# Dividing attention outputs instead of attention weights in a hybrid RWKV-7 / MLA trunk

## The chip, the cores and the metric

The kernel runs on one core of one Trainium2 chip. The core has five engines that run side by side and wait for one another through semaphores: PE (TensorE, matrix products and transposes through the array, results in PSUM), DVE (VectorE), ACT (ScalarE), POOL (GpSimd) and SP (SyncE, which here issues the DMA transfers). In the profile PEld is the loading of weights into the array, which overlaps PE's products. The metric is device time in microseconds; the time before is the median of three runs.

## The reference, cut to what matters

Two layers of a decoder trunk over 512 tokens, width 1024. Each layer projects the normed input, runs an RWKV-7 time mix and an MLA attention beside each other, gates and sums both, and adds a gated ConvFFN. The change lies in the attention of MLA, 8 heads with values of width 64:

```
def attend(args):                      # one block of 128 queries
    qn, qr, q0 = args
    s = (jnp.einsum('bqhd,bkhd->bhqk', qn, k_nope)
         + jnp.einsum('bqhr,bkr->bhqk', qr, k_pe)).astype(jnp.float32) * scale
    q_pos = q0 + jnp.arange(Q_BLOCK, dtype=jnp.int32)
    s = jnp.where(key_pos[None, :] <= q_pos[:, None], s, NEG_INF)
    p = jax.nn.softmax(s, axis=-1).astype(v.dtype)
    return jnp.einsum('bhqk,bkhd->bqhd', p, v)
...
y_b = MLA(p_B) @ w_out_mla
merged = sigmoid(gate_a) * y_a + sigmoid(gate_b) * y_b
```

## The kernel before

All activations are kept transposed: 128 features on the partitions, 512 tokens along a row. Weights stream from HBM in units of eight 128x128 tiles (raw); ACT rounds each to a high part (whi, L201) and DVE takes the rest (wlo, L202), and every large product is three matmuls of 512 columns, high by high, high by low and low by high (mm3, L246 to L248, into an accumulator acc). split (L276 to L284) makes the same two parts, hi on ACT (L279) and lo on DVE (L280), of an activation that such a product is to read.

The mixer of a layer has three stages. The first projects the input. The second is the RWKV scan over eight chunks (L777 to L815), whose matmuls on PE stand in an order written out by hand. The third, in pool tb (from L817), has six parts, listed at L952: outputs makes the four output blocks of the scan (chunk_out, L825, copied out of the PSUM tile xy on ACT, L844); norms does a group norm on each (L848 to L863: sums, subtraction and squares on DVE and ACT, the power on POOL at L858, the scaling on POOL at L863); heads(0) and heads(1) do the attention of two pairs of heads; transposed turns the normed blocks into operands of the next product (yop, L867, PE transposes at L869, then a split); heads(2) and heads(3) do the other two pairs. Behind them come eight products with the operands yops (wtile, L957, 12 matmuls each, read by DVE at L960), and after the mixer eight products with the attention operands oops (L978, read at L981).

Outside of the blocks marked manual_schedule a planner sets the order of the instructions on each engine, from the dependencies, the order of the program, its own estimate of how long each one takes, and the buffers that are free. So the engines do not run these parts one after the other: in the trace heads(0) begins among the last chunks of the scan, heads(1) runs among the group norms, and the products with yops fill gaps of heads(2) and heads(3). An engine then takes its instructions strictly in the order that the planner gave it.

heads(p) (L907 to L950) works like this. K of the pair is projected (L909) and copied for each of its two heads (L913 on ACT, L914 on POOL); q is projected and multiplied by its norm on DVE (L921). Then, for each of four blocks b of 128 queries and each head hh:

- scores on PE, 128 x n with n = 128(b+1), into the PSUM tile sc (L929);
- on DVE the scaling by -scale, the causal mask and the row's minimum (L932);
- on ACT P = exp(min - s), with the sum of the row read out into mn[:, 1:2] (L935, an ACTIVATE and a read of the accumulator);
- on DVE the reciprocal of the sum (L936), on ACT the multiplication of P by it (L937);
- on PE b+1 transposes of P into the PSUM tile pt (L940), which is copied out to PT by ACT or DVE in turn (L942);
- after both heads, on PE the products with V (L947), two per block of keys, which collect the block's 128 columns of po: the tile po is 128 x 512, its upper 64 rows one head, its lower 64 the other, its columns the tokens.

Behind the four blocks, split (L950) makes hi and lo of po for the product with oops.

The PSUM tiles of this stage are xy (twice 512 columns), two buffers of sc, two of acc, and one buffer each of pt and po, 512 columns wide.

Of the kernel before, what the change touches and what calls it, by code (L numbers as in the profile page):

```python
# [9 lines left out]
F32 = mybir.dt.float32  # L10
F32R = mybir.dt.float32r
I32 = mybir.dt.int32
AF = mybir.ActivationFunctionType
ALU = mybir.AluOpType
# [144 lines left out]
def build(ctx, tc, x, pos, wst, vecd, constd, out):  # L159
    nc = tc.nc  # L160
    V, A, G, PE = nc.vector, nc.scalar, nc.gpsimd, nc.tensor

    def pool(**kw):
        return tc.tile_pool(reuse_waits="tile", **kw)
# [4 lines left out]
    xp = ctx.enter_context(pool(name="xop", bufs=16))  # L169
# [15 lines left out]
    ident = cst[:, C_ID:C_ID + 128]  # L185
# [59 lines left out]
    def mm3(ps, w, xx, first, last):  # L245
        PE.matmul(ps, w[0], xx[0], start=first, stop=False)  # L246
        PE.matmul(ps, w[0], xx[1], start=False, stop=False)  # L247
        PE.matmul(ps, w[1], xx[0], start=False, stop=last)  # L248

    def wtile(ops):  # L250
        ps = acc()
        for i, o in enumerate(ops):
            mm3(ps, W.get(), o, i == 0, i == len(ops) - 1)
        return ps
# [16 lines left out]
    def acc():  # L271
        return accp[-1].tile([128, 512], F32, name="acc", tag="acc")

    def split(pool, src, scale, tag, bufs=None):

        hi = pool.tile([128, 512], F32R, name="hi", tag=tag, bufs=bufs)  # L276
        lo = pool.tile([128, 512], F32R, name="lo", tag=tag, bufs=bufs)
        if scale is None:
            A.copy(hi, src)  # L279
            V.tensor_tensor(lo, src, hi.bitcast(F32), ALU.subtract)  # L280
        else:
            A.activation(hi, src, AF.Copy, scale=scale)  # L282
            V.scalar_tensor_tensor(lo, src, scale, hi.bitcast(F32), ALU.mult, ALU.subtract)
        return hi, lo  # L284
# [140 lines left out]
    def mixer(l, ops, nrm, wks):  # L425
        with ExitStack() as mx:
# [208 lines left out]
            pb = mx.enter_context(pool(name=f"pb{l}", bufs=1, space=PSUM))  # L635
            mx.enter_context(accs(f"accB{l}", 2))

            def sc(name="sc"):
                return pb.tile([128, 512], F32, name=name, tag="sc", bufs=2)
# [7 lines left out]
            with pool(name=f"ti{l}", bufs=2) as ti, tc.manual_schedule(engines={PE.engine}):  # L647
# [129 lines left out]
                for c in range(8):  # L777
                    i, e = divmod(c, 2)
# [38 lines left out]
            with pool(name=f"tb{l}", bufs=2) as tb:  # L817
                def MT(name, tag, bufs=3):
                    return tb.tile([128, 512], F32, name=name, tag=tag, bufs=bufs)
# [85 lines left out]
                oops = []  # L905

                def heads(p):  # L907
                    psk = acc()
                    mm3(psk, [w[:, 128 * p:128 * p + 128] for w in lk], kvop, True, True)  # L909
                    qs, ks = [], []  # L910
                    for hh in range(2):
                        K = MT("K", "qk", 5)
                        A.copy(K[0:64, :], psk[64 * hh:64 * hh + 64, :])  # L913
                        G.tensor_copy(K[64:128, :], kp[64:128, :])  # L914
                        ks.append(K)
                    for hh in range(2):
                        psq = acc()
                        for j in range(2):
                            mm3(psq, W.get(), qops[j], j == 0, j == 1)
                        q = MT("q", "qk", 5)  # L920
                        V.tensor_tensor(q, psq, rq, ALU.mult)  # L921
                        qs.append(q)
                    po = pb.tile([128, 512], F32, name="po", tag="po")
                    for b in range(4):
                        n = 128 * (b + 1)
                        PTs = []
                        for hh in range(2):
                            sp = sc()
                            PE.matmul(sp[:, 0:n], qs[hh][:, 128 * b:128 * b + 128], ks[hh][:, 0:n], start=True, stop=True)  # L929
                            P = MT("P", "P")  # L930
                            mn = tb.tile([128, 4], F32, name="mn", bufs=4)
                            V.tensor_tensor_reduce(out=P[:, 0:n], in0=sp[:, 0:n],  # L932
                                                   in1=cst[:, C_CAUS + 512 - n:C_CAUS + 512], scale=-ATT_SCALE,
                                                   scalar=1e30, op0=ALU.add, op1=ALU.min, accum_out=mn[:, 0:1])
                            A.activation(P[:, 0:n], P[:, 0:n], AF.Exp, bias=mn[:, 0:1], scale=-1.0, accum_out=mn[:, 1:2])  # L935
                            V.reciprocal(mn[:, 2:3], mn[:, 1:2])  # L936
                            A.activation(P[:, 0:n], P[:, 0:n], AF.Copy, scale=mn[:, 2:3])  # L937
                            pt = pb.tile([128, 512], F32, name="pt", tag="pt")
                            for kb in range(b + 1):
                                PE.transpose(pt[:, 128 * kb:128 * kb + 128], P[:, 128 * kb:128 * kb + 128], ident)  # L940
                            PT = MT("PT", "PT")
                            (A.copy if b % 2 else V.tensor_copy)(PT[:, 0:n], pt[:, 0:n])  # L942
                            PTs.append(PT)
                        for kb in range(b + 1):
                            for hh in range(2):
                                hd = 2 * p + hh
                                PE.matmul(po[64 * hh:64 * hh + 64, 128 * b:128 * b + 128], Vt[:, kb, 64 * hd:64 * hd + 64],  # L947
                                          PTs[hh][:, 128 * kb:128 * kb + 128], start=kb == 0, stop=kb == b,
                                          tile_position=(0, 64 * hh))
                    oops.append(split(xp, po, None, "xb", 8))  # L950

                for f in (outputs, norms, lambda: heads(0), lambda: heads(1), transposed, lambda: heads(2), lambda: heads(3)):  # L952
                    f()
# [10 lines left out]
    for l in range(DEPTH):  # L964
# [6 lines left out]
        oops, gas = mixer(l, ops, nrm, wks)  # L971
        with pool(name=f"h{l + 1}", bufs=8, side="right") as hp, accs(f"accC{l}", 6):
            with pool(name=f"mg{l}", bufs=16, side="right") as mp:
                mops = []
                gbs = []
                for m in range(KT + 1):
                    if m < KT:
                        pb = wtile(oops)  # L978
# [25 lines left out]
            with pool(name=f"ff{l}", bufs=44) as fp:  # L1004
# [39 lines left out]
                if last:  # L1044
# [35 lines left out]
                    for j in range(2):  # L1080
                        for i in range(2):
                            o = fp.tile([128, 528], F32, name="o", tag="ft", bufs=7)[:, 0:512]
# [24 lines left out]
```

## Time and profile before

| | before |
|---|---|
| median of three runs | 1593.67 us (1593.37 to 1593.8) |
| profiled execution, its own time | 1593.16 us |
| span from its first to its last instruction | 1591.4 us |
| PE busy | 1562.6 us, 98% of the span |
| DVE busy | 915.4 us, 58% |
| ACT busy | 661.5 us, 42% |
| POOL busy | 184.7 us, 12% |

Busy time is the union of an engine's instructions. [...] The times of a row are in microseconds from the start of the span; an "idle" entry behind a row names what the engine waited for just before it. The attention of layer 0 lies at about 262 to 354 us, that of layer 1 at about 1047 to 1139 us.

### The profile page before, as it was taken

The numbers are of one execution on the slowest core, as the hardware profiler recorded it, in microseconds if no ns is written. First come the engines' busy times: TensorE is split into PE (matmuls) and PEld (weight loads), VectorE is DVE, ScalarE is ACT, GpSimd is POOL, SyncE is SP. The second block draws the span as 40 slices with busy tenths as digits, with TensorE's granted clock in tenths as the row PEclk, the third lists the DMA queues.
The fourth block names the chain that finished last, engine by engine and source line by source line (L and its number), as shares of the span: only waits on it lengthen the run. The fifth ranks groups of instructions, "written<-read, shape, count | busy, mean of one in ns | idle before, by whom it ended". The sixth has DMA issues, their size and how long they took to land.

```text
span 1591.4 us, 22441 instructions
## 1 busy us (share of the span) xinstructions
PE 1562.6 (98%) x9052; PEld 1254.2 (79%) x9052; DVE 915.4 (58%) x1468; ACT 661.5 (42%) x996; POOL 184.7 (12%) x156
## 2 busy tenths in 40 slices
PE   8999999899999999999999999998999999999998
PEld 6878886668888888888878888775788888888887
DVE  6579786666555555533346668757564655554332
ACT  6445444563443333422244443446533434333222
POOL 1011102300311101100001111013002111010000
PEclk9999999999999999999999999999999999999999
DMA  5323322224423233233343233213253332332232
GB/s 192 125 100 132 121 81 67 88 74 147 123 96 99 93 97 102 93 108 120 110 146 106 94 106 120 74 48 101 86 162 103 97 102 93 95 104 93 93 104 82
DMA packets 57272, 166.08 MB, mean 104 GB/s; under 512 B 6352, under 2 KB 8528, under 8 KB 57168
## 3 DMA queue, kind: packets, MB, share of 16 engines
q1 hardware_dynamic: 57024, 164.48, 31.9%
q8 instruction: 71, 1.16, 0.3%
q14 instruction: 33, 0.27, 0.1%
q10 hardware_dynamic: 144, 0.16, 0.0%
HBM read 147.32 MB, written 17.30 MB: 103 GB/s over the span
## 4 chain that ended last, share of the span: by engine, by line
PE 91%; DVE 4%; issue 2%; ACT 1%; POOL 1%; DMA 0%; SPq 0%; POOLq 0%; DVEq 0%; ACTq 0%
PE acc L246 26%; PE acc L247 26%; PE acc L248 26%; PE sc L929 2%; PE po L947 2%; PE pt L940 1%; PE m L599 1%; PE xy L795 1%; DVE wlo L202 1%; PE m L607 1%; PE m L583 0%; PE xy L804 0%; PE m L524 0%; DVE X L661 0%; POOL mu L858 0%
## 5 line engine op out<-in xcount | busy, mean ns | idle before, releaser
L246 PE MATMUL acc<-hi,whi 128*128 128x512 f32 (+1 forms) x1910 | 752.4, 394 | 7.2 <-ACT hi L282 5.2
L248 PE MATMUL acc<-hi,wlo 128*128 128x512 f32 (+1 forms) x1910 | 742.6, 389 | 1.2 <-DVE wlo L202 1.2
L247 PE MATMUL acc<-lo,whi 128*128 128x512 f32 (+1 forms) x1910 | 742.8, 389 | 0.0
L201 ACT CAST whi<-raw 128x1024 fp32r<-128x1024 f32 (+2 forms) x249 | 253.5, 1019 | 547.2 <-PE acc L247 466.9
L246 PEld LDWEIGHTS acc<-hi,whi 128*128 128x128 f32 x1910 | 359.6, 188 | 82.5 <-ACT hi L282 5.2
L248 PEld LDWEIGHTS acc<-hi,wlo 128*128 128x128 f32 x1910 | 359.6, 188 | 76.1 <-DVE wlo L202 1.6
L247 PEld LDWEIGHTS acc<-lo,whi 128*128 128x128 f32 x1910 | 359.9, 188 | 72.4 <-issue 1.2
L202 DVE TENSOR_TENSOR wlo<-raw,whi 128x1024 fp32r<-128x1024 f32 (+2 forms) x249 | 309.5, 1244 | 175.9 <-ACT whi L201 175.5
L1027 POOL TENSOR_TENSOR c<-c,rstd 128x512 f32<-128x512 f32 x44 | 58.0, 1318 | 403.5 <-ACT c L1026 403.5
L1020 DVE TENSOR_TENSOR u<-acc,rstd 128x512 f32<-128x512 f32 x44 | 30.4, 692 | 104.7 <-PE acc L248 104.6
L1029 DVE TENSOR_TENSOR c<-c,acc 128x512 f32<-128x512 f32 x44 | 30.3, 688 | 86.4 <-POOL c L1027 86.4
L1026 ACT ACTIVATE c<-c 128x512 f32<-128x512 f32 x44 | 27.8, 632 | 81.6 <-DVE c L1025 81.6
L305 POOL TENSOR_TENSOR nv<-nv,cst 128x4 f32<-128x4 f32 (+1 forms) x10 | 10.0, 997 | 352.6 <-DVE nv L304 352.6
L341 POOL TENSOR_TENSOR nacc<-nacc,nsq 128x512 f32<-128x512 f32 x14 | 25.0, 1787 | 200.3 <-ACT nsq L340 200.3
L450 DVE TENSOR_TENSOR cur<-acc,rstd 128x512 f32<-128x512 f32 x28 | 19.1, 690 | 48.4 <-PE acc L248 39.3
L929 PE MATMUL sc<-K,q 128*128 128x128 f32 (+3 forms) x128 | 44.6, 446 | 1.1 <-DVE q L921 1.1
L935 ACT ACTIVATE P<-P,mn 128x128 f32<-128x128 f32 (+3 forms) x64 | 35.6, 556 | 17.2 <-issue 9.3
L932 DVE CUSTOM_DVE_ANT_0 P<-sc,cst 128x128 f32<-128x128 f32 (+3 forms) x64 | 30.7, 483 | 12.9 <-PE pt L940 10.4
L947 PE MATMUL po<-PT,Vt 128*64 128x128 f32 x320 | 37.5, 286 | 0.6 <-DVE PT L942 0.6
L937 ACT ACTIVATE P<-P,mn 128x128 f32<-128x128 f32 (+3 forms) x64 | 34.2, 557 | 6.6 <-DVE mn L936 6.6
L1023 ACT ACTIVATE c<-u,vec 128x512 f32<-128x512 f32 x44 | 35.7, 812 | 2.8 <-DVE u L1019 2.8
L947 PEld LDWEIGHTS po<-PT,Vt 128*64 128x64 f32 x320 | 22.3, 136 | 18.2 <-issue 7.3
(242 smaller groups left out, 1370.8 us busy)
## 6 DMA issues: line engine op xcount, KB each, us to landing
raw<-in_w SPq DMA_DIRECT2D x238, 512.0 KB, 3.4
gate_d<-gg SPq DMA_DIRECT2D x32, 256.0 KB, 2.1
AM<-gate_d SPq DMA_DIRECT2D x16, 256.0 KB, 5.9
gb<-gate_d SPq DMA_DIRECT2D x16, 256.0 KB, 3.6
h<-in_x SPq DMA_DIRECT2D x8, 256.0 KB, 4.6
rgate_d<-gt SPq DMA_DIRECT2D x8, 256.0 KB, 2.5
bl_d<-rk SPq DMA_DIRECT2D x8, 256.0 KB, 2.0
bl<-bl_d SPq DMA_DIRECT2D x8, 256.0 KB, 2.6
```

Of the source, the lines that this page charges most:

```text
L201: A.copy(hi, r)
L202: V.tensor_tensor(lo, r, hi.bitcast(F32), ALU.subtract)
L246: PE.matmul(ps, w[0], xx[0], start=first, stop=False)
L247: PE.matmul(ps, w[0], xx[1], start=False, stop=False)
L248: PE.matmul(ps, w[1], xx[0], start=False, stop=last)
L929: PE.matmul(sp[:, 0:n], qs[hh][:, 128 * b:128 * b + 128], ks[hh][:, 0:n], start=True, stop=True)
L932: V.tensor_tensor_reduce(out=P[:, 0:n], in0=sp[:, 0:n], in1=cst[:, C_CAUS + 512 - n:C_CAUS + 512], scale=-ATT_SCALE, scalar=1e30, op0=ALU. ...
L935: A.activation(P[:, 0:n], P[:, 0:n], AF.Exp, bias=mn[:, 0:1], scale=-1.0, accum_out=mn[:, 1:2])
L937: A.activation(P[:, 0:n], P[:, 0:n], AF.Copy, scale=mn[:, 2:3])
L947: PE.matmul(po[64 * hh:64 * hh + 64, 128 * b:128 * b + 128], Vt[:, kb, 64 * hd:64 * hd + 64], PTs[hh][:, 128 * kb:128 * kb + 128], start=k ...
L1023: A.activation(cc, u[:, 2:514], AF.Identity, bias=vc(l, "conv_b", i), scale=vc(l, "conv_w", 2 * FT + i))
L1027: G.tensor_tensor(cc, cc, rstd, ALU.mult)
```

## The change

P is no longer divided. The exponentials go into the transposes as they are, and the sums of the eight rows-of-128 (four blocks, two heads) are collected in one tile, sums, column 2b+hh. Behind the product with V of the pair, the eight sums are inverted in one instruction on DVE. They lie one per token on the partitions, while po has tokens along its rows; so POOL copies each of the eight columns over 64 columns of a tile r, and four PE transposes turn r into a tile inv in which row f, column t holds the inverse for feature row f and token t. inv takes the buffer of pt. ACT copies po to a tile o, DVE multiplies o by inv, and split makes hi and lo of o, where it made them of po before. Four of this are done in each layer, one per pair of heads.

```
                     po = pb.tile([128, 512], F32, name="po", tag="po")
+                    sums = tb.tile([128, 16], F32, name="ls", bufs=2)
                     for b in range(4):
...
-                            A.activation(P[:, 0:n], P[:, 0:n], AF.Exp, bias=mn[:, 0:1], scale=-1.0, accum_out=mn[:, 1:2])
-                            V.reciprocal(mn[:, 2:3], mn[:, 1:2])
-                            A.activation(P[:, 0:n], P[:, 0:n], AF.Copy, scale=mn[:, 2:3])
+                            A.activation(P[:, 0:n], P[:, 0:n], AF.Exp, bias=mn[:, 0:1], scale=-1.0,
+                                         accum_out=sums[:, 2 * b + hh:2 * b + hh + 1])
...
-                    oops.append(split(xp, po, None, "xb", 8))
+
+                    V.reciprocal(sums[:, 8:16], sums[:, 0:8])
+                    r = MT("r", "R", 2)
+                    G.tensor_copy(r.rearrange("p (j i) -> p j i", i=64), sums[:, 8:16, None].to_broadcast([128, 8, 64]))
+                    inv = pb.tile([128, 512], F32, name="pt", tag="pt")
+                    for b in range(4):
+                        PE.transpose(inv[:, 128 * b:128 * b + 128], r[:, 128 * b:128 * b + 128], ident)
+                    o = MT("o", "R", 2)
+                    A.copy(o, po)
+                    V.tensor_tensor(o, o, inv, ALU.mult)
+                    oops.append(split(xp, o, None, "xb", 8))
...
-    nc = _bacc.Bacc("TRN2", target_bir_lowering=False, num_devices=1)
+    nc = _bacc.Bacc("TRN2", target_bir_lowering=False, num_devices=1, dynamic_dma_scratch_size=1024)
```

r and o share the tag R with two buffers of 2 KB per partition, so pool tb grows by 4 KB per partition and the small tile of sums. The last edit gives a size to a scratch area for dynamic DMA, as its name says, which was left at its default before.

## The prediction

> **What bounds the kernel now.** First the page: the busy shares and the chain of work that ended last.
>
> ```profile
> PE 1562.6 (98%) x9052; PEld 1254.2 (79%) x9052; DVE 915.4 (58%) x1468; ACT 661.5 (42%) x996; POOL 184.7 (12%) x156
> ...
> PE 91%; DVE 4%; issue 2%; ACT 1%; POOL 1%; DMA 0%; SPq 0%; POOLq 0%; DVEq 0%; ACTq 0%
> ```
>
> PE is the bound of the whole. But the share is a mean, so next the busy times by stage, cut where attention begins, where the scan ends, where PE is full again and where attention ends (the same in layer 1 for the second of them).
>
> ```profile
> core 0: us, PE busy (x) PEld busy (x) DVE busy (x) ACT busy (x) POOL busy (x), PEclk, DMA share, GB/s
> ...
> 262.00:284.50 22.50, 22.34 (x233) 15.39 (x232) 13.46 (x40) 11.23 (x29) 2.02 (x4) 1.00 0.06 22
> 284.50:313.00 28.50, 24.38 (x341) 16.99 (x341) 20.86 (x57) 17.28 (x40) 12.98 (x11) 1.00 0.33 104
> 313.00:354.00 41.00, 41.00 (x241) 27.09 (x241) 24.47 (x75) 27.87 (x69) 0.76 (x1) 1.00 0.24 73
> ...
> 1070.00:1098.50 28.50, 24.39 (x341) 16.95 (x340) 20.93 (x57) 17.40 (x41) 12.99 (x11) 1.00 0.32 104
> ```
>
> Three different stages. From 262 to 284.5 (heads(0) among the scan) PE is full but for 0.16 us. From 284.5 to 313 (group norms and heads(1)) it idles 28.50 - 24.38 = 4.12 us, and 4.11 in layer 1: 8.23 us in all, the most that the change can win without taking work from PE. From 313 to 354 (heads(2), heads(3), products with yops between them) PE never idles, and ACT is busy 27.87 of 41 us without holding anybody. What ended PE's waits around layer 0's attention (waits of PE, 255 to 365 us):
>
> ```profile
> engine line waited for: us in total, times, longest us
> PE xy L869 <- POOL Z L863: 1.2, 1, 1.2
> PE pt L940 <- DVE mn L936: 0.7, 1, 0.7
> PE xy L833 <- ACT Z L844: 0.7, 2, 0.3
> PE xy L869 <- ACT Z L844: 0.6, 1, 0.6
> PE sc L929 <- DVE q L921: 0.5, 1, 0.5
> PE po L947 <- DVE PT L942: 0.3, 1, 0.3
> PE pt L940 <- ACT P L937: 0.2, 1, 0.2
> ```
>
> They sum to 4.2 us. 2.5 of them (Z, three rows) are the group norm and the copies of the scan's output, which the change doesn't touch. Only the two rows of pt name the division. The larger is not what it says (instructions in order of time):
>
> ```profile
> 309.65 0.56 DVE L942 COPY PT<-pt 128x384 f32<-128x384 f32 x1 [1.31 <-PE pt L940]
> 310.13 0.15 DVE L936 RECIPROCAL mn<-mn 128x1 f32<-128x1 f32 x1
> ...
> 310.36 0.52 PE L940 MATMUL pt<-cst,P 128*128 128x128 f32 x3 [0.74 <-DVE mn L936]
> ```
>
> The transposes need the one buffer of pt, and that is free when the copy ends at 310.21; the reciprocal just ends after it. So the division itself holds PE 0.2 us in a layer by this table, the round trip through pt 0.7.
>
> **The change part by part.** *Removed*: 64 scalings on ACT and 64 reciprocals on DVE.
>
> ```profile
> L937 ACT ACTIVATE P<-P,mn 128x128 f32<-128x128 f32 (+3 forms) x64 | 34.2, 557 | 6.6 <-DVE mn L936 6.6
> ...
> L936 DVE RECIPROCAL mn<-mn x64: 139/158/165, 266.3 to 1133.9; 128x1 f32<-128x1 f32 x64
> ```
>
> ACT loses 34.2 us, DVE 64 x 0.158 = 10.1 us, and PE no instruction. Each softmax loses a chain of about 0.16 + 0.56 us. Behind it a PE that is full hides that, so it is worth nothing from 313 on; where a stall goes there, the next thing late is PE itself.
>
> *Added, four times a layer, eight times in all*. On the other engines, from like instructions:
>
> ```profile
> L921 DVE TENSOR_TENSOR q<-acc,rq 128x512 f32<-128x512 f32 x8 | 5.5, 687 | 2.3 <-PE acc L248 2.3
> ...
> L942 ACT COPY PT<-pt 128x512 f32<-128x512 f32 x8 | 4.7, 587 | 6.4 <-PE pt L940 6.4
> ...
> L897 POOL CAST lk<-whi x2: 613/613/613, 255.0 to 1040.4; 128x512 fp32r<-128x512 f32 x2
> ...
> L511 POOL CAST lw<-whi x2: 1667/1668/1669, 29.7 to 813.9; 128x512 fp32r<-128x512 f32 x2
> ...
> L863 POOL TENSOR_TENSOR Z<-Z,mu x8: 1043/1045/1097, 292.1 to 1089.6; 128x512 f32<-128x512 f32 x8
> ```
>
> The inversion of 128x8 0.17 us, as a little more than L936's 128x1, and the product with inv 0.69 on DVE, 8 x 0.86 = 6.9 (DVE wins 3.2 net); the copy of po 0.59 on ACT, 8 x 0.59 = 4.7 (ACT wins 29.5 net); split stays, with o in the place of po. The broadcast on POOL isn't in the trace: 0.61 us as the plain copy, 1.05 as the broadcast product, 1.67 at worst; I take 0.61, the same shape with one input, and keep 1.67 for the range. POOL is busy 0.76 of 41 us from 313 on, and among the group norms 12.98 of 28.5, so it has room.
>
> On PE four transposes of 128x128. Groups of four stand in the chain of work that ended last, which gives the time that they hold PE:
>
> ```profile
> 312.40 0.59 PE pt L940 x4
> ...
> 314.12 0.44 PE pt L940 x4
> ...
> 349.22 0.59 PE pt L940 x4
> ...
> 351.20 0.44 PE pt L940 x4
> ```
>
> 0.44 to 0.59, mean 0.52 (the higher where they follow the products with V). Eight groups: 3.5 to 4.7 us, I take 8 x 0.5 = **4.0**. If those of heads(0) and heads(1) fall into PE's idle time, only four count, 1.8. [...]
>
> *Moved*. No DMA is issued, removed or reordered in the program, and neither SP's nor POOL's queue has a transfer in it that the new instructions pass by: the broadcast on POOL stands behind the group norm's, the rest in the queues of ACT and DVE where split stood. The scratch size changes no instruction; every transfer of the list of issues leaves from SP's queue, so I cost it at nothing.
>
> *New waits*. The chain at a pair's end grows: inversion, broadcast and transposes run beside the last copy to PT and the products with V, then come the copy to o 0.59, the product 0.69, hi and lo. The reader is far away: the last lo of po is over at 355.3, the first product with oops at 369.8, and its 12 matmuls of some 0.23 us begin at about 367.
>
> ```profile
> 354.57 0.69 DVE L280 TENSOR_TENSOR lo<-po,hi 128x512 fp32r<-128x512 f32 x1 [2.64 <-ACT hi L279]
> ...
> 369.85 0.69 DVE L981 SCALAR_TENSOR_TENSOR gb<-gb,acc 128x512 f32<-128x512 f32 x1 [0.63 <-PE acc L248]
> ```
>
> 1.3 us more there are covered by some 12. po comes free earlier (one copy, not hi and lo). pt is what is held longer, see the second rival. If r is late, the transposes wait, and all of PE's queue behind them: up to 1.67 - 0.61 = 1.1 us a time where the planner reckons with the short one.
>
> *Won*. The softmax of heads(0) and heads(1) becomes shorter, so PE has work ready earlier in the stretch with 4.12 us idle. 0.2 of it is the division's, 2.5 the group norm's; the other 1.5 (pt, PT, q) hang on loaded ACT and DVE queues. I take 1.0 us per layer, **2.0** in all; bounds 0 and 8.2.
>
> Sum against the profiled execution: 1593.16 + 4.0 - 2.0 = 1595.2. The median of the runs before is 0.5 above that execution, so 1595.7 by the median, and I give **1595.5**. One term has no sign: the planner makes a new order for all of PE's stream here. A change of kind costs, as the first matmul of 512 columns after another kind shows against the next:
>
> ```profile
> 353.91 0.43 PE acc L246
> 354.34 0.24 PE acc L247
> ```
>
> 0.2 us each; ten switches more or less in a layer, of over a hundred, give 4 us in all to either side.
>
> **The rivals.** *Faster*: ACT with 30 us less lets heads(1) fill the whole idle stretch, and the four groups of that stretch lie in it too. 8.2 - 4.0 = 4.2 won, 1589.0 (1589.5 by the median). For it: ACT waits 2.2 us for L936 there and DVE sits 0.9 us behind pt. Against it: 2.5 of 4.12 us hang on the group norm, and where PE is full the transposes are pure addition.
>
> *Slower*: the single buffer of pt. Before, it was free with the copy to PT. Now inv sits in it from the transposes until DVE's product, which waits for the products with V (1.09 us) and the copy to o (0.59), then takes 0.69: some 2.5 us with the signals. The next pair can't transpose in that time. Last group of one pair and first of the next, in PE's list:
>
> ```profile
> 286.14 0.66 PE L940 MATMUL pt<-cst,P 128*128 128x128 f32 x4
> ...
> 301.61 0.27 PE L940 MATMUL pt<-cst,P 128*128 128x128 f32 x1
> ...
> 313.96 0.60 PE L940 MATMUL pt<-cst,P 128*128 128x128 f32 x4
> ...
> 320.22 0.27 PE L940 MATMUL pt<-cst,P 128*128 128x128 f32 x1
> ...
> 335.56 0.60 PE L940 MATMUL pt<-cst,P 128*128 128x128 f32 x4
> ...
> 337.64 1.09 PE L947 MATMUL po<-PT,Vt 128*64 128x128 f32 x14
> ...
> 338.66 0.33 PE L940 MATMUL pt<-cst,P 128*128 128x128 f32 x1
> ```
>
> 15 us, 6 us and 2.5 us lie between, so only the third handover is tight: products over at 338.7, copy and product until 340.2, the next transposes 1.5 us late, and there products with yops stand ready. It decides where the planner has nothing to put between, or reckons the release too early. With 1.5 us at each of six handovers and nothing won: 1593.2 + 4.0 + 9 = 1606; at two of them 1600, which I take for this case. [...]
>
> *Nothing of it matters*: transposes and gain cancel, 1593.7; this lies inside the forecast's own range, 1592 to 1598.
>
> **How the numbers follow.** Forecast 1592 to 1598: 0.62. Faster, around 1589.5: 0.13. Slower by the handovers or late broadcasts, around 1600: 0.25. The range reaches to both: 1590 to 1601, with the unsigned 4 us in it. 0.2% is 3.2 us, about what a measurement of this kernel can tell from no change: below 1590.5 is faster, above 1596.9 slower. The upper fifth of the forecast lies over that line, so slower is 0.25 + 0.09, about 0.34; faster 0.13; within 0.53.
>
> **What would show it.** PE's instructions grow by 32 to 9084, and its busy time by about what the time grows less the idle won; ACT falls to about 632 us, DVE to 912, POOL grows to about 190. The stretch from the scan's end to full PE keeps 3 us of its 4.1 us idle. Groups of four transposes of r hold PE about 0.5 us, with no wait before them longer than some tenths. It is wrong if PE waits for r or for pt by whole microseconds (then slower), if idle time in that stretch nearly goes (then faster), or if the broadcast on POOL takes over 1.7 us.

## The result, and the profile after

| | before | after |
|---|---|---|
| median | 1593.24 us (1591.73 to 1593.8, six runs) | 1601.5 us (1599.73 to 1605.42, six runs) |
| ratio | | 1.0056, 95% interval 1.0043 to 1.0069 |
| profiled execution, own time / span | 1593.16 / 1591.4 us | 1605.42 / 1603.6 us |
| mean granted clock of it | 0.997 | 0.992 |

The change makes the kernel slower, by 8.3 us in the median. The forecast was 1595.5 and the range ended at 1601, with a chance of 0.34 for slower; the time lies half a microsecond outside the range. The profiled execution of the new kernel is the slowest of its six, 3.9 us above their median; that matters below.

The page of the new kernel, its busy shares and the chain of work that ended last:

```profile
PE 1574.0 (98%) x9084; PEld 1263.4 (79%) x9084; DVE 915.9 (57%) x1420; ACT 637.8 (40%) x940; POOL 191.7 (12%) x164
...
PE 91%; DVE 5%; issue 2%; ACT 1%; POOL 0%; DMA 0%; DVEq 0%; POOLq 0%; SPq 0%; ACTq 0%
```

PE's 32 new instructions are there, and ACT lost 23.7 us. But PE is busy 11.4 us longer, far more than the 32 transposes take (4.7 us, at the 0.59 for four below). The stages show why (stretch, length, then busy us and instructions of PE, PEld, DVE, ACT, POOL; the eighth figure is PE's granted clock):

```profile
core 0: us, PE busy (x) PEld busy (x) DVE busy (x) ACT busy (x) POOL busy (x), PEclk, DMA share, GB/s
284.50:313.00 28.50, 24.14 (x289) 16.06 (x285) 19.44 (x49) 13.88 (x32) 13.12 (x10) 0.94 0.30 94
313.00:354.00 41.00, 40.47 (x254) 27.17 (x254) 25.39 (x65) 22.95 (x55) 3.54 (x5) 1.00 0.18 52
...
1070.00:1098.50 28.50, 24.15 (x369) 18.09 (x367) 17.72 (x40) 11.56 (x24) 11.42 (x9) 0.91 0.28 94
```

Against the same stretches before, the group norms keep all of their idle time (4.36 us, 4.12 before), the stretch behind them, full before, has 0.53 us of it, and the clock, 1.00 in the group norms of both layers before, is 0.94 and 0.91. (The group norms of layer 1 begin 6.7 us later than before; in a window moved by that the clock is 0.88.) The waits of PE from 262 to 360 us:

```profile
engine line waited for: us in total, times, longest us
PE xy L869 <- POOL Z L863: 2.1, 1, 2.1
PE sc L930 <- DVE q L921: 1.4, 1, 1.4
PE xy L833 <- ACT Z L844: 0.7, 2, 0.4
PE po L947 <- DVE PT L942: 0.5, 1, 0.5
```

The rows that named the division are gone, and nothing waits for r or for pt. But the wait for the scaled Z grew from 1.2 to 2.1 us and that for q from 0.5 to 1.4. They stand close together (PE's list):

```profile
297.69 0.49 PE L930 MATMUL sc<-K,q 128*128 128x128 f32 x2 [1.39 <-DVE q L921]
...
300.99 0.33 PE L869 MATMUL xy<-cst,Z 128*128 128x128 f32 x1 [2.10 <-POOL Z L863]
...
303.29 0.63 PE L247 MATMUL acc<-lo,whi 128*128 128x512 f32 x1
303.72 0.63 PE L248 MATMUL acc<-hi,wlo 128*128 128x512 f32 x1
```

Between 296.30 and 300.99, PE waits 3.49 us, and right behind it products of 512 columns start 0.43 us apart (their rows, 0.63 us long, overlap by 0.20), where the chain before had 0.24. Windows of 4 us show the same by the granted clock:

```profile
296.00:300.00 4.00, 1.49 (x7) 0.71 (x5) 4.00 (x12) 1.98 (x6) 2.31 (x3) 1.00 0.01 2
300.00:304.00 4.00, 3.01 (x9) 2.35 (x10) 1.17 (x5) 0.15 (x1) 1.38 (x2) 0.67 0.41 131
304.00:308.00 4.00, 4.00 (x17) 1.83 (x16) 1.76 (x7) 2.32 (x8) 2.24 (x2) 0.90 0.01 4
```

PE is busy 1.49 of the first 4 us, while DVE is busy in all of them; the clock falls in the next window. So the question becomes what DVE was doing (list of DVE):

```profile
292.38 0.68 DVE L959 TENSOR_TENSOR o<-o,pt 128x512 f32<-128x512 f32 x1
292.97 0.17 DVE L853 TENSOR_SCALAR mu<-mu 128x8 f32<-128x8 f32 x1
293.05 0.69 DVE L921 TENSOR_TENSOR q<-acc,rq 128x512 f32<-128x512 f32 x1
293.65 0.68 DVE L854 TENSOR_TENSOR Z<-Z,mu 128x512 f32<-128x512 f32 x1
294.25 1.54 DVE L280 TENSOR_TENSOR lo<-o,hi 128x512 fp32r<-128x512 f32 x1
...
296.96 0.68 DVE L921 TENSOR_TENSOR q<-acc,rq 128x512 f32<-128x512 f32 x1
```

The product and the split of heads(0) sit in the middle of the group norms' own steps on DVE (L852 to L857). The product is 0.68 us, as reckoned. lo is 1.54 us, where lo of po took 0.69 (0.68 at 293.99 us, where it stood among the group norms before, too). It now reads two operands in SBUF, o and hi; before, one of them was po in PSUM. Beside it, POOL (its list, the scaling and the copy of K):

```profile
293.67 1.57 POOL L863 TENSOR_TENSOR Z<-Z,mu 128x512 f32<-128x512 f32 x1
295.30 0.96 POOL L914 COPY K<-kp 64x512 f32<-64x512 f32 x1
```

The scaling took 1.04 to 1.10 us before, and this copy of K 0.61. So both engines lose time. lo starts 0.58 us behind the start of the scaling and ends 0.55 us behind its end; the copy of K starts beside lo. The scaling itself starts 0.02 us behind the group norm's subtraction (L854), which also has two operands in SBUF; e4 and e10 below tell this one from lo. Among DVE's rows, the product o by inv, with one operand in PSUM, kept its 0.68 us, and in e10 lo with one operand in PSUM took 0.69 beside the same scaling. Two operands in SBUF alone were not slow: the other three lo of o in layer 0, with no instruction of POOL beside them, took 0.68 to 0.69 us, as did the four of e6 in layer 0 (0.68 in the mean), where the work comes later. So lo was long where both came together, two operands in SBUF and POOL's instructions beside it; by what means, no run shows.

The theory to test: heads(0)'s added work on DVE, its lo at 1.54 us beside POOL's instructions, makes q and Z late; PE waits; the granted clock falls for some microseconds. Rivals: pt, the sum of the transposes alone, the planner's new order whatever is added, the scratch size.

### The profile page after: what moved, and what is told of

It reads as the page before. It is cut to its first block, busy times and chain, and to the rows that moved or that the text cites. A ratio compares the mean times of both kernels' runs of the same rounds, so it can differ in the third digit from the quotient of the medians.

```text
span 1603.6 us, 22449 instructions
## 1 busy us (share of the span) xinstructions
PE 1574.0 (98%) x9084; PEld 1263.4 (79%) x9084; DVE 915.9 (57%) x1420; ACT 637.8 (40%) x940; POOL 191.7 (12%) x164
## 4 chain that ended last, share of the span: by engine, by line
PE 91%; DVE 5%; issue 2%; ACT 1%; POOL 0%; DMA 0%; DVEq 0%; POOLq 0%; SPq 0%; ACTq 0%
PE acc L246 26%; PE acc L247 26%; PE acc L248 26%; PE sc L930 2%; PE po L947 2%; PE pt L940 1%; PE m L599 1%; PE xy L795 1%; DVE wlo L202 1%; PE m L607 1%; PE m L583 0%; PE xy L785 0%; PE xy L804 0%; PE m L524 0%; DVE X L661 0%
## 5 line engine op out<-in xcount | busy, mean ns | idle before, releaser
L936 ACT ACTIVATE P<-P,mn 128x128 f32<-128x128 f32 (+3 forms) x64 | 35.9, 560 | 42.8 <-DVE mn L933 37.5
L1035 DVE SCALAR_TENSOR_TENSOR c<-u,vec,c 128x512 f32<-128x512 f32 x44 | 33.1, 752 | 1.5
```

What stands on the lines that cost most here:

```text
L1035: V.scalar_tensor_tensor(cc, u[:, 0:512], vc(l, "conv_w", i), cc, ALU.mult, ALU.add)
```

## The experiments

Each experiment stands against runs of the kernel before on the same chip (medians 1592.81 us for e1 to e4, 1591.41 for e5 to e8, 1592.07 for e9 to e11).

**Which pair?** Pairs not in LATE keep the division of P and the split of po as before.

```
+LATE = (2, 3)          # e1; (0, 1) in e2, (0,) in e5, (1,) in e9
...
+                            if p in LATE:
                                 A.activation(..., accum_out=sums[:, 2 * b + hh:2 * b + hh + 1])
+                            else:
+                                A.activation(..., accum_out=mn[:, 1:2])
+                                V.reciprocal(mn[:, 2:3], mn[:, 1:2])
+                                A.activation(P[:, 0:n], P[:, 0:n], AF.Copy, scale=mn[:, 2:3])
...
+                    if p not in LATE:
+                        oops.append(split(xp, po, None, "xb", 8))
+                        return
```

Pairs 2 and 3 alone, expected:

> The division is moved behind the V product for heads(2) and heads(3) only; heads(0) and heads(1) scale P as before. Theory T: the loss comes from the tail of heads(0) (product with inv, hi, lo) among the group norms, where DVE's queue makes PE wait for q (1.4 us) and for Z (2.1 us) and the granted clock then falls; the late pairs only pay for four groups of four transposes, about 1.8 us. So 1594 to 1596 us, clock 1.0 through both attention stages, no wait of PE above 1.2 us. Rival R: the loss is PE's added work and the longer hold of pt, alike for all four pairs; half of 8.3 us, 1597 to 1598.

Pairs 0 and 1 alone, expected:

> The division is moved for heads(0) and heads(1) only; heads(2) and heads(3) scale P as before. Theory T: nearly all of the loss is here, 1599 to 1601 us, with PE's waits for q and Z of 1.4 and 2.1 us as in the changed kernel and a granted clock below 1 behind them in both layers. Rival R: half of the loss, 1597 to 1598.

Measured: e1 1594.18 us, ratio 1.0008 (0.9999 to 1.0017); e2 1599.99 us, 1.0042 (1.003 to 1.0054). The loss lies in the first two pairs. In e1 the stages of layer 0 are those of before: PE 24.40 of 28.5 and 41.00 of 41 us, clock 1.00. e2 has the waits of the new kernel, 2.1 us for Z and 1.4 for q. Then each of the two alone:

> The division is moved for heads(0) only. Theory T (DVE's share of the tail of heads(0), above all lo with two SBUF inputs beside POOL, delays the group norms and with them q and Z): the wait for q of 1.4 us is there, lo takes over 1 us, and most of the 7.2 us of the kernel with pairs 0 and 1 appear: 1597 to 1599 us. If instead each pair pays alike for its own transposes and hold of pt, a quarter of 8.3 us: 1594.5 to 1595.5.

> Only the pair of heads(1) is changed, in both layers; the other three pairs divide P as before. Two groups of four transposes cost 2 x 0.45 = 0.9 us. Theory (the loss comes from the extra work of heads(0), whose product and split fall among the group norms, with one wait for Z of 2.1 us and one for q of 1.4 us, and a lower granted clock behind them): heads(1) ends behind the group norms, so its split reads o at about 0.69 us, waits of PE stay as before (none above 1.2 us), granted clock 1.00 from 284.5 to 313, time +0.5 to +2 us over before. Rival (any pair among the first two brings a new order that holds Z late): +6 us or more, Z 2.1 us, clock 0.94.

Measured: e5 1602.45 us, 1.0066 (1.0052 to 1.008), so heads(0) alone brings the whole loss, more than I expected: 11.0 us, where pairs 0 and 1 together cost 7.2 and all four 8.3. Why one pair costs more than all stays open. e9 1594.71 us, 1.0014 (1.0006 to 1.0023), 2.6 us over before where 0.5 to 2 were expected. Waits of PE in e5, and its row of lo among the groups by shape:

```profile
PE xy L870 <- POOL Z L864: 2.1, 1, 2.1
PE sc L931 <- DVE q L922: 1.4, 1, 1.4
```

```profile
L281 DVE TENSOR_TENSOR lo<-o,hi 128x512 fp32r<-128x512 f32 x1 | 1.5, 1531 | 0.0
```

In e9 the attention of layer 0 has no wait above 1.0 us and is shorter than before (the table below). What its profiled execution loses, it loses between DVE's first read of a product with oops in layer 0 and the first copy of Z in layer 1: 704.65 us (369.65 to 1074.30), where before has 701.80 (369.85 to 1071.65). In that stretch lies the scan of layer 1, with a low clock (windows of e9):

```profile
1000.00:1047.00 47.00, 44.20 (x597) 33.95 (x596) 31.03 (x53) 18.65 (x26) 3.57 (x6) 0.93 0.26 91
```

The profiled execution of the new kernel has 0.89 in that window, before 1.00, and from the one point to the other it takes 705.63 us (372.70 to 1078.33): 3.8 more than before, about what it stands above its own median. What sets the clock down in the scan stays open. Over the thirteen traces this stretch takes from 700.4 to 705.6 us, and not by the waits of the attention: e2, which has those of the new kernel, has 700.41, e9, which has none above 1.0 us, 704.65. So a difference of a few us between two medians can't be put down to the attention without its trace.

**Is it the division that is missed, or the new order?** e3 leaves the division out altogether, both the old one and everything added for the new one.

```
-                    V.reciprocal(sums[:, 8:16], sums[:, 0:8])
...
-                    V.tensor_tensor(o, o, inv, ALU.mult)
-                    oops.append(split(xp, o, None, "xb", 8))
+                    oops.append(split(xp, po, None, "xb", 8))
```

> Leaves the division out: P goes on undivided as in the changed kernel, and po is split without being multiplied; no inversion, broadcast, transposes, copy to o or product. It shows what taking the division out of the softmax is worth by itself. Theory T: the removal is not what costs; 1591 to 1593.5 us, clock 1.0, PE's waits in the group-norm stretch no longer than before (4.1 us in a layer). Rival P: it is the planner's new order of PE's stream, brought about by the shorter softmax, that opens the waits; then they stay (1.4 and 2.1 us) and the time is 1597 or above.

Measured: 1593.06 us, 1.0004 (0.9995 to 1.0013). The removal is worth nothing that can be told from no change, even with no price to pay for it. The trace says more (windows of e3, the group norms of both layers):

```profile
284.50:313.00 28.50, 24.83 (x302) 16.68 (x303) 19.99 (x49) 14.51 (x34) 12.90 (x11) 1.00 0.33 103
...
1070.00:1098.50 28.50, 24.88 (x307) 16.40 (x303) 18.79 (x47) 13.37 (x31) 12.91 (x11) 0.94 0.28 93
```

The idle time shrinks by 0.45 us only, from 4.12 to 3.67: the wait for Z is 2.7 us in two pieces, the longest again 2.1. So that wait comes with the planner's new order alone, once heads(0) is over earlier. And the two layers, equal in busy time, differ in the clock.

**Is it the two SBUF operands of lo?** In e4 the product is written back into inv, in PSUM, and split reads it there; e10 does so with heads(0) alone.

```
-                    V.tensor_tensor(o, o, inv, ALU.mult)
-                    oops.append(split(xp, o, None, "xb", 8))
+                    V.tensor_tensor(inv, o, inv, ALU.mult)
+                    oops.append(split(xp, inv, None, "xb", 8))
```

> The whole change, but DVE writes the product with inv back into the PSUM tile inv and split reads it there, so that lo has one input from SBUF and not two; pt is held until lo is done. Theory T in its sharp form: lo among the group norms took 1.54 us instead of 0.68 since it ran beside POOL's scaling with both inputs in SBUF, and POOL's scaling 1.57 instead of 1.04; with this lo takes 0.7 us again, the waits for q and Z shrink by about 1 us and the clock holds: 1595 to 1598 us. If the slow lo is not what matters, 1600 to 1603 us, and more if the longer hold of pt costs.

> Only the pair of heads(0) is changed, and the product is written back into inv in PSUM, from which split reads, so that lo has one operand in SBUF and one in PSUM as before the change. With the product in SBUF this pair alone took 11.0 us more than before. Theory (contention of lo with POOL's scaling is half of the delay, the planner's order the other half): lo takes 0.69 us instead of 1.54, the wait for q falls from 1.4 to about 0.5, that for Z stays at about 2 us, the clock stays above 0.96, time +2 to +6 us. Rival (contention is all): time within 2 us of before and no wait for Z above 1.2 us. Second rival (it is nothing): +9 us or more.

Measured: e4 1597.02 us, 1.003 (1.002 to 1.0041); e10 1599.3 us, 1.0043 (1.0031 to 1.0055), against 1.0066 for the same pair with the product in SBUF. Waits of e10, and its lists of DVE and of POOL (the subtraction and lo, the scaling and the copy of K):

```profile
PE xy L870 <- POOL Z L864: 2.1, 1, 2.1
PE pt L946 <- DVE mn L942: 0.7, 1, 0.7
PE xy L834 <- ACT Z L845: 0.7, 2, 0.4
PE sc L931 <- DVE q L922: 0.5, 1, 0.5
```

```profile
294.07 0.68 DVE L855 TENSOR_TENSOR Z<-Z,mu 128x512 f32<-128x512 f32 x1
294.67 0.69 DVE L281 TENSOR_TENSOR lo<-pt,hi 128x512 fp32r<-128x512 f32 x1
```

```profile
294.09 1.56 POOL L864 TENSOR_TENSOR Z<-Z,mu 128x512 f32<-128x512 f32 x1
295.72 0.61 POOL L915 COPY K<-kp 64x512 f32<-64x512 f32 x1
```

lo is back at 0.69 us and q at 0.5, and about a third of the loss is gone: 7.2 us over before, where e5 had 11.0. The slow lo is real and not the whole; the time missed my 2 to 6 us, and the clock stayed at 0.94 and 0.88 with the wait for Z at 2.1 us. The time of e4 lies in the range that I gave, but not all of the theory held: lo took 0.69 us and the wait for q was 0.5, while that for Z stayed at 2.1, and the clock held in one layer only (0.94 and 1.00). In e10 the copy of K is back at 0.61 us, but POOL's scaling still takes 1.56 us, with lo reading PSUM. In e4 POOL's ten instructions from 284.5 to 313 us take 12.76 us, 0.36 less than the ten of the new kernel; the copy of K, at 0.61 for 0.96, would make 0.35 of it and leave the scaling as long as it was. So it isn't lo that lengthens the scaling. In e10 it starts 0.02 us behind the subtraction of the group norm, in the new kernel 0.02 (layer 0) and 0.03 (layer 1); that the subtraction holds it up fits these rows, but no run moves the subtraction alone.

**Does it go away when the tail of heads(0) and heads(1) comes later?** In e6 the copy to o stays where it was, and the broadcast, transposes, product and split of the first two pairs are written behind transposed. o and r no longer share a tag: o has two buffers of its own, r one.

```
-                for f in (outputs, norms, lambda: heads(0), lambda: heads(1), transposed, lambda: heads(2), lambda: heads(3)):
-                    f()
+                outputs()
+                norms()
+                tails = [heads(0), heads(1)]
+                transposed()
+                for t in tails:
+                    t()
+                heads(2)()
+                heads(3)()
```

> The whole change, but the tails of heads(0) and heads(1) behind the copy to o (broadcast, transposes, product, hi, lo) are written behind the part transposed, so that the planner puts them behind the group norms. Theory T: the product and the slow lo leave the group norms, lo takes 0.7 us, PE's wait for q falls below 0.6 us; the wait for Z of 2.1 us can stay, since the kernel without division had it too; 1595 to 1598 us. If DVE's work in that stretch is not the cause, 1600 to 1603 us.

Measured: 1593.4 us, 1.0009 (1.0 to 1.0018), better than I expected. All 32 transposes are in it. Its windows:

```profile
284.50:313.00 28.50, 25.79 (x320) 17.88 (x317) 21.09 (x53) 14.82 (x35) 13.30 (x11) 1.00 0.36 113
313.00:354.00 41.00, 40.99 (x245) 27.33 (x244) 24.39 (x62) 21.96 (x55) 2.44 (x4) 1.00 0.20 62
```

The idle time falls to 2.71 us, the longest wait for Z is 1.0, and the clock is full. Putting both edits together was to show whether the place of the product still matters (diffs of e6 and e4 together):

> All four pairs changed; the work behind the copy to o of heads(0) and heads(1) is written behind transposed, and the product is written back into inv in PSUM, from which split reads. Theory: with the tails behind the group norms the contention is already gone (lo took 0.68 us there), so the place of the product adds nothing: the same as with the deferred tails alone, +1 to +3 us over before, clock 1.00, no wait for Z above 1.1 us. Rival: pt is held longer (until hi and lo are over, some 1.4 us more), so that the next transposes wait at the tight handovers: +4 us or more, with waits for pt named in PE's list.

Measured: 1597.16 us, 1.0034 (1.0022 to 1.0046): the rival. Now pt is held until hi and lo are over, and PE waits for it (waits of e11, 262 to 360 us):

```profile
PE xy L869 <- POOL Z L863: 1.7, 2, 1.0
PE pt L940 <- DVE PT L942: 0.8, 1, 0.8
PE pt L940 <- DVE lo L280: 0.7, 1, 0.7
```

**What is the idle time worth if PE is given work in it?** e7 adds eight products to each layer ahead of the transposes of Z, whose results are overwritten.

```
+                        if p == 0:
+                            for _ in range(8):
+                                PE.matmul(ps[:, 1, :], ident, Z[:, 1, 0, :], start=True, stop=True)
```

> The whole change, with eight products of 512 columns in fp32 per layer added (the identity with Z's block 1, into the half of xy that is written over afterwards), some 0.43 us of PE each, 6.9 us in all; the planner spreads them over the stretch of heads(1), and the transposes of Z come behind them. Theory T: PE's idle time (over 4 us a layer) and the lost clock are worth more than the added work: no wait of PE above 1 us in that stretch, clock 1.0 there, and no more than the changed kernel's time, 1597 to 1601 us. Rival: idle time and clock cost little and PE's added work is what counts, as with the transposes: 1606 to 1609 us.

Measured: 1604.49 us, 1.008 (1.0067 to 1.0094), between the two. The filler is larger than I had reckoned, since each product is two instructions (page and chain of e7):

```profile
PE 1579.1 (99%) x9116; PEld 1262.7 (79%) x9116; DVE 915.7 (57%) x1420; ACT 637.3 (40%) x940; POOL 190.7 (12%) x164
```

```profile
298.53 0.86 PE xy L891 x2
```

32 more by 0.43 us are 13.8 us in all. The idle time of the stretch is 1.39 us, the clock 1.00 in both layers. 13.8 of filler and 4.7 of transposes less 2 x 2.73 of idle give 13.0; measured are 13.1. So nothing else is lost in this run, with the clock at 1.00. By what it adds, though, it can't win.

**The scratch size** alone, on the kernel before:

> The kernel before with only the last edit of the change, the scratch size of 1024. It issues no DMA that would need it, by the list of queues: 1592 to 1594 us as before. If the scratch slowed transfers, PE's waits for weights at the start would grow and the time exceed 1595.

Measured: 1592.1 us, 1.0003 (0.9994 to 1.0011), no change that the runs can tell.

**The sum, kernel by kernel.** The attention stage of layer 0, from the start of ACT's first copy of Z (L844 before) to the start of DVE's first read of a product with oops (L981 before), is 83.56 us before (286.29 to 369.85). In the table, idle is 69.5 us less PE's busy time from 284.5 to 354; a group of four transposes is 0.59 us, as the chain of the new kernel has it:

```profile
318.06 0.59 PE pt L956 x4
```

| kernel | stage, layer 0 | longer | groups x 0.59 | idle, against 4.12 | remainder | clock 284.5 to 313 |
|---|---|---|---|---|---|---|
| after | 88.02 | 4.46 | 2.36 | +0.77 | 1.3 | 0.94 |
| e1, pairs 2, 3 | 84.53 | 0.97 | 1.18 | -0.02 | -0.2 | 1.00 |
| e2, pairs 0, 1 | 87.72 | 4.16 | 1.18 | +1.02 | 2.0 | 0.94 |
| e3, no division | 83.75 | 0.19 | 0 | -0.45 | 0.6 | 1.00 |
| e4, product in PSUM | 86.60 | 3.04 | 2.36 | -0.55 | 1.2 | 0.94 |
| e5, pair 0 | 87.18 | 3.62 | 0.59 | +1.03 | 2.0 | 0.94 |
| e6, tails later | 84.43 | 0.87 | 2.36 | -1.40 | -0.1 | 1.00 |
| e7, filler (6.9) | 90.02 | 6.46 | 2.36 | -2.73 | -0.1 | 1.00 |
| e9, pair 1 | 83.15 | -0.41 | 0.59 | -0.80 | -0.2 | 1.00 |
| e10, pair 0 in PSUM | 86.44 | 2.88 | 0.59 | +0.20 | 2.1 | 0.94 |
| e11, e6 and e4 | 86.04 | 2.48 | 2.36 | +0.05 | 0.1 | 1.00 |

The remainder is the stage's growth less the two terms (and less the filler). It is 0 within 0.2 us where the clock is full, but for e3, and 1.2 to 2.1 where it is 0.94; 28.5 x 0.06 = 1.7 us of clock are missing there. e3 and e4 give the same price within one kernel: the layer with 0.94 has a stage 1.57 us longer in e3 (85.32 to 83.75) and 1.53 in e4 (86.60 to 85.07) than the layer with 1.00.

For the whole kernel: 8 x 0.59 = 4.7 us of transposes, 2 x 0.77 = 1.5 of idle and 2 x 1.3 = 2.7 of clock make 8.9, against 8.3 in the medians. This takes layer 0 of the profiled execution twice; layer 1 of it, at the lower clock, is 5.40 us longer than before (88.97 against 83.57).

No version here beats the kernel before: what is removed buys nothing (e3), and 4.7 us of transposes stand against at most 2 x 1.4 us of idle time won (e6).

## Why the prediction was wrong

- *What bounds the kernel, and what the removal is worth.* Right. e3 removes the division for nothing and gains nothing.
- *The transposes, 4.0 us.* Mis-sized: 4.7. The upper end of the rows was the right one, since these groups stand behind the products with V, as the prediction itself said of the 0.59. (Its 1.8 us for four groups is at 0.45 each; by its own 0.5 they would be 2.0.)
- *The other engines, costed at nothing.* **This is the step that failed**: "split stays, with o in the place of po", and POOL "has room". The DVE that was to hide it had to serve the group norm in that stretch: product and lo of heads(0) stand ahead of steps on which Z and q hang, in all 2.22 us where lo alone took 0.68 (by line and tile, DVE's 1420 instructions start in the trace of the new kernel in the order in which the program lists them). With this work behind the group norms (e6) the kernel is 2.0 us over before instead of 8.3; with lo reading PSUM (e4) it is 4.2 over. The wait for q follows lo: 1.4 us in the new kernel, e2 and e5, 0.5 in e4 and e10. The wait for Z of 2.1 us does not: it is there in e4 and e10, and in e3, which has none of the added work. In e3 it comes with the planner's new order alone; why the order of e6 has only 1.0 stays open. And lo with both operands in SBUF isn't the lo of before. That could be read in the trace of before, in a like instruction with two SBUF operands, wlo from raw and whi:

```profile
L202 DVE TENSOR_TENSOR wlo<-raw,whi x249: 414/1225/2942, 4.6 to 1561.7; 128x1024 fp32r<-128x1024 f32 x118, 128x256 fp32r<-128x256 f32 x4, 128x512 fp32r<-128x512 f32 x3
```

Its median is 1.23 us and its maximum 2.94. One of the longer ones stands in this very stretch, beside POOL's scaling (lists of DVE and of POOL of the kernel before):

```profile
299.78 1.79 DVE L202 TENSOR_TENSOR wlo<-raw,whi 128x1024 fp32r<-128x1024 f32 x1
```

```profile
299.45 1.04 POOL L863 TENSOR_TENSOR Z<-Z,mu 128x512 f32<-128x512 f32 x1
```

I had taken the duration of lo from a row with an operand in PSUM.
- *Won, 2.0 us.* Not in this kernel: the idle time grew by 1.5. Even with nothing added (e3) it falls by 0.45 us in layer 0, not by 1.0, since the wait for Z grows. But e6, which keeps the work out of the way, won 2.8, and 4.7 - 2.8 = 1.9 us is what it measures over before (2.0). The forecast's net sum, 4.0 - 2.0, is near that of e6 since both of its terms are some 0.7 to 0.8 us short.
- *The granted clock* had no term. It fell where two waits of 1.4 and 2.1 us came within 5 us, and also where that for Z of 2.1 us stood with one of 0.5 or less for q (e10, and one layer each of e3 and e4). In the profiled execution of the new kernel it cost 1.3 us in layer 0 and 2.3 in layer 1, by the remainders.
- *The new order, plus or minus 4 us for changes of kind.* No such term is needed: the remainders at full clock are 0.2 us or less, but for e3. What the order did change is which wait stands where.
- *The slower rival, pt.* Its time was nearest, for a reason that isn't there: nobody waits for pt after the change. The mechanism exists, and e11 shows its price where pt is held longer: 0.7 us behind lo and 0.8 behind the copy to PT in layer 0, neither of which e6 has.
- *The counts.* PE's 9084 instructions and no wait for r were right. DVE (915.9 for 912), ACT (637.8 for 632) and POOL (191.7 for 190) came out a little above; the broadcast on POOL took the 0.61 us assumed in the median, 0.96 at most. The 3 us of idle expected in the stretch were 4.36.

## What to carry to other kernels

Before work on an engine with a low share is costed at nothing, look at whose steps stand behind it in that engine's queue in that very stretch: with 0.68 and 1.54 us on DVE, 57% busy over the whole, moved out of the group norms (e6), the loss was 2.0 us and not 8.3, a larger difference than the 4.7 us of 32 transposes on PE. When an operand moves from PSUM to SBUF, take the duration from a row with the same places of its operands, and read its maximum beside its median. And when a change only shifts waits together, look at the granted clock before explaining a longer busy time by more work.

## What was unexpected in the hardware

- **DVE and POOL beside each other.** lo of 128x512 with both operands in SBUF took 1.54 us beside POOL's scaling, and the copy of K beside it 0.96 instead of 0.61; with one operand in PSUM lo took 0.69 beside the same scaling and the copy 0.61, and with its tail deferred lo took 0.68 (e6, layer 0). The scaling took 1.56 to 1.57 instead of 1.04 to 1.10 where it started 0.02 to 0.03 us behind a subtraction on DVE with two operands in SBUF, with lo reading SBUF (new kernel) or PSUM (e10).
- **The clock fell on a mostly full stream.** Before, waits of at most 1.2 us left it at 1.00 in the profiled attention stages; after waits of 1.4 and 2.1 us within 5 us it fell, to 0.67 in the lowest window of 4 us, and products of 512 columns went from 0.24 to 0.43 us apart; in e10 waits of 0.5 and 2.1 us were enough for 0.94 and 0.88 in the group norms. In the new kernel PE had idled 3.49 of 4.69 us, in two pieces of which the longer is 2.10 us. What decides it is not shown: in e3 and e4 the two layers, with all but equal busy time in the stretch (24.83 and 24.88 us, 25.00 and 25.01), got 1.00 in one and 0.94 in the other.
- **The time of a run follows it.** The six runs of the new kernel go from 1599.73 us at a mean clock of 0.996 to 1605.42 at 0.992, and the twelve of e4 from 1592.68 at 0.998 to 1600.6 at 0.994: 1.4 to 2 us for each 0.001. How far the runs of a kernel spread does not follow its waits: e5, which has both of the long ones, spreads over 2.9 us in five runs, e9, which has none above 1.0 us, over 6.8 in twelve.
